# A decoder layer on one core: ordered first statistics in twelve 92-token tiles, three buffers moved, a 256-token last block

## The chip, the cores and the metric

The kernel runs on one core of a Trainium2 chip. A core has TensorE (PE in the profile, with its weight loads as PEld), VectorE (DVE), ScalarE (ACT), GpSimd (POOL) and SyncE (SP), which issues the DMAs here; 16 DMA engines move the data. The metric is device microseconds for one launch: lower is better. Clock means the clock that was granted to TensorE, 1.00 for 2.4 GHz and 0.50 for 1.2 GHz.

## The reference

One decoder layer over 1104 tokens: 16 learned meta tokens and a prompt of 1024 tokens (one sequence of 1040), and 8 sampled sequences of 8 tokens. The model is 1024 wide.

```python
def decoder_layer(x, st, p):
    x = x + 0.5 * swiglu(rmsnorm(x, p['ffn1_norm']), p['ffn1_w_gu'], p['ffn1_w_down'])   # 1024 -> 2 x 2816 -> 1024
    u = rmsnorm(x, p['mix_norm'])
    z = u @ p['w_in']
    # A gated DeltaNet, B S5 (complex diagonal state), C RG-LRU, D GLU + causal depthwise conv31 + LayerNorm; each 256 wide
    ...
    gates = jax.nn.sigmoid(zg.reshape(*zg.shape[:-1], N_BRANCH, D_MODEL))
    x = x + jnp.sum(gates * proj, axis=-2) @ p['w_out']
    x = x + 0.5 * swiglu(rmsnorm(x, p['ffn2_norm']), p['ffn2_w_gu'], p['ffn2_w_down'])
```

y_prompt (without the meta tokens) and y_sample are the RMSNorm of x with final_norm. The new states of the four branches are outputs too.

## The kernel before

Activations lie with the 1024 (or 2816) channels on the partitions and tokens along the free dimension. Every float32 product is made of three passes of a narrower type (hi times hi, hi times lo, lo times hi), so a weight tile `raw` is split by a cast on ACT into `whi` and a subtraction on DVE into `wlo`, and so are the activations. The framework's scheduler sets the order on each engine by its own simulation of the times; `high_priority` and `issue_after` steer it. On each engine, and on SP's queue, instructions then run in that order, and one that waits holds back all that stand behind it. A pool tile has a tag and a number of buffers; a new tile of a tag waits until an old one is no longer read.

The stages are FFN 1, the norm of the mixers (`norms`), the input projection with the four branches woven into it, the merge, FFN 2 and the final norm.

- **Start of FFN 1.** The input arrives with tokens on partitions, in ten tiles: 16 meta tokens, eight of 128 tokens and one of 64. PE turns each in eight transposes (`turn_x`, into `xs`), and ACT or DVE sum the squares of each row (`stats_x`, with an rsqrt and three Newton steps on DVE: `rsqrt_rows`). PE spreads the row factors `y` over all partitions into `rs`. `scale` multiplies by `rs` and the norm weight, and a split into hi and lo gives the factor `b` that the matmuls read. FFN 1 works in token blocks of 276; the first one needs tokens from four tiles, the first four loaded. The gate and up products of the first four units (of 128 of the 2816 channels) are made plainly, for the token blocks 0 and 1: units 0 and 1, then 2 and 3, each pair 96 matmuls for a block. All later work uses seven products of sums for every eight (`a_prep` adds the weights, `b_first` and `b_rest` the activations). `a_prep` takes three raw tiles, `r1`, `r2` and `s23`, of which the last two come from the pool `gw` with two buffers.
- **norms** keeps two accumulators per token block of 368, one of them a `raw` tile of the weight pool. The first tile of w_in is loaded into the next free `raw`.
- **Delta rule (branch A).** `scale_q` is called for three token blocks and multiplies the queries `a_qe` by decays that a DMA spreads over the partitions into `a_bc`: two rows of 368 numbers, each to 64 partitions, 184 KB. It does so twice for a block, six times in all, on POOL. `a_bc` shares its one buffer (tag `n_acc0`) with other work, `b_sg` of S5 among it. A chunk of the rule takes `a_mt`, `a_tk` from DRAM, `a_wT` from ACT and `a_kd` from POOL.
- **Conv (branch D)** multiplies by a tap on ACT into `d_tmp` (one buffer) and adds on POOL into `d_acc`.
- **S5 (branch B)** has four steps q; each does input matmuls (`b_mi`), a scan on DVE, and output matmuls (`b_H` with `b_mo`). A `yield` lets a piece of the input projection (24 matmuls of 368 columns) go between.
- **down** adds the last group of units' outputs in three token blocks of 368; after each, `final` transposes the tokens of that block back, three outputs of up to 128 tokens, and normalises and stores them. The third output of each block uses the tile `fy`, with one buffer.

Of the kernel before, what the change touches and what calls it, by code (L numbers as in the profile page):

```python
# [13 lines left out]
D = 1024  # L14
# [12 lines left out]
NS = 276  # L27
NF = DFF // 128
# [14 lines left out]
class Kernel:  # L43
# [52 lines left out]

    def split(self, hi, lo, x, eng=None):
        self.nc.scalar.copy(out=hi, in_=x)  # L98
        (eng or self.nc.vector).tensor_tensor(out=lo, in0=x, in1=hi.bitcast(F32), op=SUB)  # L99

    def rsqrt_rows(self, ps, out, tmp):

        nc = self.nc
        nc.scalar.activation(out=out, in_=ps, func=AF.Abs_reciprocal_sqrt, bias=self.eps[:ps.shape[0]])
        nc.vector.scalar_tensor_tensor(out=tmp, in0=ps, scalar=EPS, in1=out, op0=ADD, op1=MULT)
        nc.vector.scalar_tensor_tensor(out=tmp, in0=tmp, scalar=-0.5, in1=out, op0=MULT, op1=MULT)
        nc.vector.scalar_tensor_tensor(out=out, in0=tmp, scalar=1.5, in1=out, op0=ADD, op1=MULT)

    def norms(self, key, after=None, tbs=range(3)):
# [166 lines left out]
    def tokens(self):  # L276

        I = self.I
        blocks = [(I["meta_tokens"], NMETA, 0)]
        for i in range(8):  # L280
            blocks.append((I["x_prompt"][0, 128 * i:128 * i + 128], 128, NMETA + 128 * i))
        return blocks + [(I["x_sample"].rearrange("b t d -> (b t) d"), TS, TP)]

    def load_x(self, tiles, pools):

        ts = []
        for i, n in enumerate(tiles):
            src, r, c0 = self.tokens()[n]
# [3 lines left out]
            ts.append((xin[:, i % 2], r, c0))  # L292
        return ts

    def turn_x(self, ts, xs, pools, tags, eng):

        nc = self.nc
        for t, r, c0 in ts:
            for h in range(2):
# [4 lines left out]
                for b in range(c0 // NS, (c0 + r - 1) // NS + 1):  # L304
                    if b not in xs:
                        xs[b] = self.slot(pools[b], "xs", F32, (8, NS))
                    lo, hi = max(c0, NS * b), min(c0 + r, NS * (b + 1))
                    dst, src = xs[b][:, 4 * h:4 * h + 4, lo - NS * b:hi - NS * b], ps[:, :, lo - c0:hi - c0]
                    if h and eng:
                        nc.vector.tensor_copy(out=dst, in_=src)  # L310
                    else:
                        nc.scalar.copy(out=dst, in_=src)

    def stats_x(self, ts, pool, tag):
# [5 lines left out]
        for i, (t, r, c0) in enumerate(ts):  # L320
            if pool and i % 2 == 0:
                junk = self.slot(pool, "junk", F32, (2, D))
            sq = junk[:r, i % 2] if pool else t[:r]
            if i == 1 and c0 < NS:
# [13 lines left out]
        nc.scalar.activation(out=self.rs[:, ts[0][2]:ts[0][2] + n], in_=ps[:, :n], func=AF.Copy, scale=float(D))  # L338
# [18 lines left out]
    def scale(self, dst, src, b, ks=range(8)):  # L357

        for k in ks:
            self.nc.vector.scalar_tensor_tensor(out=dst(k), in0=src(k), in1=self.rs[:, NS * b:NS * (b + 1)], op0=MULT,  # L360
                                                scalar=self.prm[:, self.po[self.gkey] + k:self.po[self.gkey] + k + 1], op1=MULT)
# [41 lines left out]
    def a_parts(self, f, rs):  # L403

        pool, out = (self.wp, self.gw)[f % 2], []
        for r in rs:
            h, l = (pool.tile([128, 8, 128], F32R, tag=x, name=x, bufs=3 if pool is self.wp else None) for x in ("whi", "wlo"))
            self.split(h, l, r)
# [28 lines left out]
    def gate_up(self, w_in, parts):  # L437
# [60 lines left out]
        def plain(f, A, t, ea):  # L498
# [9 lines left out]
            for i in range(2):  # L508
                product(ps[i], A[i][1], B[6 if t else 1], False)
                with self.tc.high_priority():  # L510
                    if t:
                        nc.vector.tensor_tensor(out=g[:, i], in0=ps[i], in1=ea[i], op=ADD)
                    if i == 0:
                        nc.scalar.activation(out=g[:, 0], in_=g[:, 0] if t else ps[0], func=AF.Silu)
# [10 lines left out]
        with self.tc.high_priority():  # L525
# [1618 lines left out]
```

## Time and profile before

| | us |
|---|---|
| Median of 3 runs | 2610.69 (2607.91 to 2612.38) |
| Profiled execution, its own time | 2605.56 |
| Its span in the profile | 2603.9 |
| PE busy | 2531.2 (97%), mean clock 0.981 |
| DVE, ACT, POOL busy | 1458.5, 912.7, 534.7 |

The profiled execution took 1.66 us more than its span, and lies 5.13 us under the median. Times in the trace are counted from the start of the span.

### The profile page before, as it was taken

The numbers are of one execution on the slowest core, as the hardware profiler recorded it, in microseconds if no ns is written. First come the engines' busy times: TensorE is split into PE (matmuls) and PEld (weight loads), VectorE is DVE, ScalarE is ACT, GpSimd is POOL, SyncE is SP. The second block draws the span as 40 slices with busy tenths as digits, with TensorE's granted clock in tenths as the row PEclk, the third lists the DMA queues.
The fourth block names the chain that finished last, engine by engine and source line by source line (L and its number), as shares of the span: only waits on it lengthen the run. The fifth ranks groups of instructions, "written<-read, shape, count | busy, mean of one in ns | idle before, by whom it ended". The sixth has DMA issues, their size and how long they took to land.

```text
span 2603.9 us, 43522 instructions
## 1 busy us (share of the span) xinstructions
PE 2531.2 (97%) x17474; PEld 2459.5 (94%) x17474; DVE 1458.5 (56%) x2729; ACT 912.7 (35%) x1665; POOL 534.7 (21%) x578
## 2 busy tenths in 40 slices
PE   7999999999999999989999999999999999999997
PEld 7999999999998898888989999999999999999997
DVE  6645444656787459687744335343855444464545
ACT  7433333421224355334523213132533333341203
POOL 1222222200002021144443222221232222210000
PEclk8999999999999999989989999999999999999999
DMA  7222222542413243633433536242222222362211
GB/s 230 77 76 92 76 76 76 199 145 82 127 68 108 78 79 121 135 97 109 128 111 97 189 101 216 87 136 93 72 87 92 76 79 79 101 216 83 103 48 69
DMA packets 317224, 280.68 MB, mean 108 GB/s; under 512 B 62708, under 2 KB 276078, under 8 KB 316886
## 3 DMA queue, kind: packets, MB, share of 16 engines
q1 hardware_dynamic: 317021, 277.90, 34.8%
q8 instruction: 137, 2.24, 0.4%
q14 instruction: 66, 0.53, 0.1%
HBM read 196.31 MB, written 81.72 MB: 107 GB/s over the span
## 4 chain that ended last, share of the span: by engine, by line
PE 83%; DVE 7%; DMA 4%; ACT 3%; issue 2%; POOL 1%; SPq 1%; POOLq 0%; DVEq 0%; ACTq 0%
PE ps_mm L59 63%; PE ps_pre L59 7%; PE ps_vn L59 6%; PE ps_o L59 6%; DVE wlo L99 1%; PE ps_P L59 1%; PE ps_pre L67 1%; DMA a_bc<-qsP 0%; DVE d_acc L783 0%; DVE b L99 0%; DVE b_t L1650 0%; ACT whi L98 0%; DVE x L578 0%; DMA tokS<-a_tok 0%; DMA raw<-in_ffn_w_gu 0%
## 5 line engine op out<-in xcount | busy, mean ns | idle before, releaser
L59 PE MATMUL ps_mm<-u,whi 128*128 128x368 f32 (+1 forms) x2816 | 719.1, 336 | 8.5 <-ACT whi L98 4.3
L59 PE MATMUL ps_mm<-h,whi 128*128 128x368 f32 x2112 | 529.2, 332 | 3.7 <-DVE x L578 3.5
L59 PEld LDWEIGHTS ps_mm<-u,whi 128*128 128x128 f32 x2816 | 504.2, 191 | 23.4 <-issue 5.7
L98 ACT CAST whi<-raw 128x1024 fp32r<-128x1024 f32 (+2 forms) x305 | 299.5, 986 | 607.6 <-PE ps_mm L59 414.8
L59 PE MATMUL ps_mm<-u,wlo 128*128 128x368 f32 (+1 forms) x1408 | 469.4, 334 | 0.0
L59 PE MATMUL ps_mm<-b,whi 128*128 128x276 f32 x2816 | 447.9, 291 | 6.3 <-ACT b L98 3.2
L99 DVE TENSOR_TENSOR wlo<-raw,whi 128x1024 fp32r<-128x1024 f32 (+2 forms) x305 | 387.0, 1273 | 102.9 <-ACT whi L98 102.1
L59 PEld LDWEIGHTS ps_mm<-b,whi 128*128 128x128 f32 x2816 | 393.3, 189 | 7.8 <-ACT b L98 3.8
L59 PEld LDWEIGHTS ps_mm<-h,whi 128*128 128x128 f32 x2112 | 374.0, 188 | 7.4 <-DVE x L578 6.2
L59 PE MATMUL ps_mm<-h,wlo 128*128 128x368 f32 x1056 | 349.4, 332 | 0.0
L59 PEld LDWEIGHTS ps_mm<-u,wlo 128*128 128x128 f32 x1408 | 268.0, 190 | 3.4 <-issue 2.0
L578 DVE SCALAR_TENSOR_TENSOR x<-ps_mm,x 128x368 f32<-128x368 f32 x288 | 154.4, 538 | 173.3 <-PE ps_mm L59 172.0
L59 PE MATMUL ps_mm<-b,wlo 128*128 128x276 f32 x1408 | 237.6, 290 | 0.0
L59 PEld LDWEIGHTS ps_mm<-b,wlo 128*128 128x128 f32 x1408 | 201.4, 189 | 0.1
L59 PEld LDWEIGHTS ps_mm<-h,wlo 128*128 128x128 f32 x1056 | 198.3, 188 | 0.3
L144 DVE TENSOR_TENSOR g_sg<-ps_mm,rs 128x368 f32<-128x368 f32 x96 | 51.8, 539 | 202.0 <-PE ps_mm L59 201.8
L427 POOL TENSOR_TENSOR raw<-raw 128x512 f32<-128x512 f32 x44 | 57.2, 1301 | 519.0 <-DVE wlo L99 499.7
L59 PE MATMUL ps_pre<-b,whi 128*128 128x276 f32 x896 | 145.5, 291 | 0.0
L59 PEld LDWEIGHTS ps_pre<-b,whi 128*128 128x128 f32 x896 | 127.1, 190 | 0.0
L1821 ACT ACTIVATE g_sg<-g_sg 128x368 f32<-128x368 f32 x96 | 48.9, 509 | 211.3 <-DVE g_sg L144 211.3
L466 DVE TENSOR_TENSOR e_g<-ps_pre,e_a 128x276 f32<-128x276 f32 x80 | 35.4, 443 | 154.6 <-DMA hS<-e_g 133.7
L489 POOL TENSOR_TENSOR e_g<-e_g,e_u 128x276 f32<-128x276 f32 x80 | 99.2, 1240 | 77.2 <-issue 35.3
(488 smaller groups left out, 3385.1 us busy)
## 6 DMA issues: line engine op xcount, KB each, us to landing
raw<-in_ffn_w_gu SPq DMA_DIRECT2D x104, 512.0 KB
raw<-in_w_in SPq DMA_DIRECT2D x50, 512.0 KB
h<-hS SPq DMA_DIRECT2D x44, 552.0 KB
hS<-e_g SPq DMA_DIRECT2D x80, 276.0 KB
raw<-in_ffn_w_down SPq DMA_DIRECT2D x38, 512.0 KB
x<-xS SPq DMA_DIRECT2D x24, 552.0 KB
mgS<-g_mg SPq DMA_DIRECT2D x24, 552.0 KB
g_b<-brS SPq DMA_DIRECT2D x16, 552.0 KB
```

The lines of the kernel that those rows point to most:

```text
L59: self.last_mm = self.nc.tensor.matmul(out=out, lhsT=lhsT, rhs=rhs, start=start, stop=stop, **kw).ins
L67: self.last_mm = self.nc.tensor.transpose(out=out, in_=in_, identity=self.ident[:n, :n]).ins
L98: self.nc.scalar.copy(out=hi, in_=x)
L99: (eng or self.nc.vector).tensor_tensor(out=lo, in0=x, in1=hi.bitcast(F32), op=SUB)
L144: self.last_dve = self.nc.vector.tensor_tensor(out=out, in0=ps, in1=r, op=MULT).ins
L427: nc.gpsimd.tensor_tensor(out=s23[:, k2], in0=r1[:, k1], in1=r2[:, k1], op=SUB)
L466: add(out=g[:, 0], in0=gam, in1=e["a"], op=ADD)
L489: nc.gpsimd.tensor_tensor(out=g[:, 1], in0=g[:, 1], in1=e["u"], op=MULT)
L578: nc.vector.scalar_tensor_tensor(out=x[:, m, sl], in0=ps, scalar=0.5, in1=x[:, m, sl], op0=MULT, op1=ADD)
L1821: self.last_act = nc.scalar.activation(out=sg, in_=sg, func=AF.Tanh, scale=0.5).ins
```

## The change

Seven edits, in the order of the program.

1. The input's 1104 tokens come in twelve tiles of 92, three to a block of 276 (`tokens`, `load_x`). The first of them is a load of 16 and one of 76 tokens, the last one of 28 and one of 64. The first block's three tiles are loaded first, then the first unit's weights, three tiles, the second unit's weights, and the last six tiles.
2. The statistics are ordered: `issue_after` keeps the splits of the first two units' weights, the second block's transposes and the first silu behind steps of the statistics. `y` itself, spread over 128 columns, is the stationary operand of the matmul that gives `rs`; the diagonal matrices go away, and so does the factor 1024. The first factor is made in two halves. The second block's rows are turned and its statistics made while the first block is at work (`next_rows`). Half of the last six tiles' copies go to DVE, and their statistics come in two groups of three.
3. `s23` of the first seven-product unit comes from the pool `wp` with the other raw tiles.
4. `norms` takes both accumulators from the pool `tp`, and no `raw`.
5. `a_bc` has a tag, and so a buffer, of its own.
6. S5: the two scan tiles become one that shares its buffer with `b_y`; one of the yields moves from ahead of the input matmuls to ahead of the output matmuls (1 and 4 in place of 2 and 3).
7. The last group of FFN 2's down product ends its blocks at tokens 400, 848 and 1104; `final` has 3, 4 and 2 outputs for them, two buffers of `fy`, and cycles through five PSUM places.

```diff
+NT = NS // 3
...
-                acc = [self.raw([128, NB]),
-                       pool.tile([128, NB], F32, tag="f_s", name="n_acc")]
+                acc = [pool.tile([128, NB], F32, tag="f_s", name="n_acc") for _ in range(2)]
...
+        xp, xs = I["x_prompt"][0], I["x_sample"].rearrange("b t d -> (b t) d")
+        c = NT * n - NMETA
+        out = []
+        if c < 0:
+            out.append((I["meta_tokens"], 0))
+        a, b = max(c, 0), min(c + NT, TP - NMETA)
+        out.append((xp[a:b], a - c))
+        if b < c + NT:
+            out.append((xs, b - c))
+        return out
...
-            self.nc.sync.dma_start(out=xin[:r, i % 2], in_=src)
+            for src, o in self.tokens(n):
+                self.nc.sync.dma_start(out=xin[o:o + src.shape[0], i % 2], in_=src)
...
-            dg = self.tp.tile([128, 128], F32, tag="f_h", name="xdg")
-            nc.scalar.activation(out=dg[:r, :r], in_=self.ident[:r, :r], func=AF.Copy, scale=y[:r, i:i + 1])
-            self.mm(ps[:, n:n + r], self.onesD[:r], dg[:r, :r])
+            self.mm(ps[:, n:n + r], y[:r, i:i + 1].to_broadcast([r, 128]), self.ident[:r, :r])
...
-            self.split(h, l, r)
+            with self.after(*b):
+                self.split(h, l, r)
...
-            r1, r2, s23 = (self.raw([128, 8, 128], pool) for pool in (None, self.gw, self.gw))
+            r1, r2, s23 = (self.raw([128, 8, 128], pool) for pool in (None, self.gw, None if f == self.NP else self.gw))
...
-        blocks = [[(16, 128), (144, 128), (272, 96)], [(368, 128), (496, 128), (624, 112)],
-                  [(736, 128), (864, 128), (992, 112)]][tb]
+        blocks = [[(16, 128), (144, 128), (272, 128)], [(400, 128), (528, 128), (656, 128), (784, 64)],
+                  [(848, 128), (976, 128)]][tb]
...
-            yt = self.raw([128, 2, 512]) if i < 2 else fp.tile([128, 2, 512], F32, tag="fy", name="fy")
+            yt = self.raw([128, 2, 512]) if i < 2 else fp.tile([128, 2, 512], F32, tag="fy", name="fy", bufs=2)
...
-                bc = self.np.tile([128, NB], F32, tag="n_acc0", name="a_bc")
+                bc = self.np.tile([128, NB], F32, tag="a_bc", name="a_bc")
...
-            yield
-            Sr, Si = (pool.tile([128, 2, NBLK], F32, tag=f"b_S{m}", name="b_S") for m in range(2))
+            S = pool.tile([128, 2, 2, NBLK], F32, tag="b_S", name="b_S")
+            Sr, Si = S[:, 0], S[:, 1]
...
-            ys = pool.tile([128, 4, NBLK], F32, tag="b_y", name="b_y")
+            ys = pool.tile([128, 4, NBLK], F32, tag="b_S", name="b_y")
             early = inputs(q + 1) if q < 3 else None
-            yield
-            yield
-            yield
+            for _ in range(4):
+                yield
...
+                    us["rs"], us["mm"], us["st"] = self.last_rs, self.last_mm, (self.last_rt, self.last_nr)
+                    self.hold = [(us["st"], (self.last_rs, self.last_nr))]
...
+                def next_rows():
+                    ts = us["ts"]
+                    with self.after(us["scaled"], us["rs"], us["mm"]):
+                        self.turn_x(ts, xs, [v] * 4, ("P", "o"), True)
+                    with self.after(*us["st"]):
+                        self.stats_x(ts, up, "vn")
...
-                    self.down(I["ffn2_w_down"], start, None, self.final)
+                    self.down(I["ffn2_w_down"], start, None, self.final, (400, 848, T))
```

The scheduler sets the order anew. On PE, this is the end of the first statistics and the first FFN matmuls in the kernel before (`ps_vn` is the spreading of the row factors; a `DMAHW` in the brackets is the load that the row waits for).

```order
L59 MATMUL ps_vn<-xdg,onesD 128x16 [waits Activation_49]
L59 MATMUL ps_vn<-xdg,onesD 128x128 [waits Activation_49] x3
L67 MATMUL ps_P<-ident,xin 128x128 [waits DMAHW5_49,PE_49,Activation_49]
L67 MATMUL ps_P<-ident,xin 128x128 x3
L67 MATMUL ps_o<-ident,xin 128x128 [waits DVE_49]
L67 MATMUL ps_o<-ident,xin 128x128 x3
L67 MATMUL ps_P<-ident,xin 128x128 [waits DMAHW6_49,Activation_49]
L67 MATMUL ps_P<-ident,xin 128x128 x3
L59 MATMUL ps_mm<-b_244,whi 128x276 [waits Activation_49]
```

And in the changed kernel:

```order
L60 MATMUL ps_vn<-ident,x_s 128x92 [waits DVE_49]
L60 MATMUL ps_vn<-ident,x_s 128x92 x2
L68 MATMUL ps_P<-ident,xin 128x92 [waits DMAHW1_49,PE_49]
L68 MATMUL ps_P<-ident,xin 128x92 x3
L68 MATMUL ps_o<-ident,xin 128x92 x4
L68 MATMUL ps_P<-ident,xin 128x92 [waits DMAHW2_49,Activation_49]
L68 MATMUL ps_P<-ident,xin 128x92 x3
L60 MATMUL ps_mm<-b_216,whi 128x276 [waits Activation_49]
```

In both, transposes of later tiles stand ahead of the first FFN matmul: in the changed kernel those of the fourth tile and half of the fifth.

On POOL, the first two multiplications by `a_bc` of the kernel before stand together ahead of the conv's additions, and the other four far behind:

```order
L1238 TENSOR_TENSOR a_qe<-a_qe,a_bc 128x368 [waits DMAHW3_49,DMAHW2_49,DMAHW4_49,DMAHW1_49,DMAHW6_49,DVE_49,Activation_49]
L1238 TENSOR_TENSOR a_qe<-a_qe,a_bc 128x368 [waits DMAHW3_49]
L797 TENSOR_TENSOR d_acc<-d_acc,d_tmp 128x368 [waits Activation_49] x2
L797 TENSOR_TENSOR d_acc<-d_acc,d_tmp 128x304 [waits Activation_49]
```

In the changed kernel the last four are these, and two more stand shortly ahead of them:

```order
L1260 TENSOR_TENSOR a_qe<-a_qe,a_bc 128x368 [waits DMAHW7_49]
L1291 TENSOR_TENSOR a_kd<-a_tk,a_kdT 40x256 [waits DMAHW6_49,PE_49]
L1260 TENSOR_TENSOR a_qe<-a_qe,a_bc 128x368 [waits DMAHW0_49]
L1260 TENSOR_TENSOR a_qe<-a_qe,a_bc 128x368 [waits DMAHW4_49,DMAHW3_49]
L1260 TENSOR_TENSOR a_qe<-a_qe,a_bc 128x368 [waits DMAHW6_49,DMAHW5_49]
L819 TENSOR_TENSOR d_acc<-d_acc,d_tmp 128x368 [waits DVE_49,Activation_49]
L819 TENSOR_TENSOR d_acc<-d_acc,d_tmp 128x368 [waits Activation_49]
```

All six stand within a stretch of 17 of POOL's rows now, among additions of the conv. On ACT of the changed kernel, the taps that these additions take stand as follows (the second row here waits for the first addition that stands behind the four multiplications):

```order
L818 ACTIVATE d_tmp<-d_buf,prm_5929 128x368 [waits Pool_49]
L1302 COPY a_vn<-ps_vn 40x256 [waits PE_49]
L818 ACTIVATE d_tmp<-d_buf,prm_5929 128x368 [waits Pool_49]
L818 ACTIVATE d_tmp<-d_buf,prm_5929 128x304 [waits Pool_49]
L818 ACTIVATE d_tmp<-d_buf,prm_5929 128x64
L1842 ACTIVATE g_sg<-g_sg 128x368 [waits DVE_49]
L1324 COPY a_qe<-ps_o 128x2x40 [waits PE_49]
L1332 COPY a_wT<-ps_pre 128x80 [waits PE_49]
```

Behind them stand a gate (`g_sg`), and `a_wT`, which PE's next chunk of the delta rule reads.

## Rows read from the trace of the kernel before

**Rows 1.** Page, busy time of an engine, share of the span and instructions.

```profile
PE 2531.2 (97%) x17474; PEld 2459.5 (94%) x17474; DVE 1458.5 (56%) x2729; ACT 912.7 (35%) x1665; POOL 534.7 (21%) x578
```

**Rows 2.** Stretches: length; PE, PEld, DVE, ACT, POOL busy; clock, DMA share, GB/s.

```profile
60.00:80.00 20.00, 20.00 (x156) 19.71 (x155) 18.91 (x30) 9.03 (x16) 1.69 (x1) 1.00 0.27 79
80.00:100.00 20.00, 16.09 (x110) 15.87 (x110) 15.20 (x16) 9.70 (x13) 8.46 (x5) 0.86 0.11 36
800.00:820.00 20.00, 15.70 (x76) 15.15 (x76) 11.89 (x19) 6.95 (x13) 7.15 (x24) 0.83 0.45 117
1220.00:1240.00 20.00, 15.79 (x106) 15.20 (x104) 11.18 (x18) 7.85 (x15) 8.59 (x10) 0.95 0.41 119
1240.00:1260.00 20.00, 19.28 (x109) 18.77 (x110) 12.20 (x18) 9.89 (x20) 9.17 (x11) 0.88 0.38 116
```

**Rows 3.** Timeline of PE, 24 to 100: start, length; in brackets idle before.

```profile
25.32 1.16 PE L59 MATMUL ps_mm<-b,whi 128*128 128x276 f32 x4
...
44.30 1.29 PE L59 MATMUL ps_mm<-b,whi 128*128 128x276 f32 x4 [3.16 <-ACT b L98]
...
59.58 0.76 PE L59 MATMUL ps_mm<-b,whi 128*128 128x276 f32 x4
...
95.19 1.28 PE L59 MATMUL ps_vn<-b,whi 128*128 128x276 f32 x4 [3.91 <-ACT whi L98]
```

**Rows 4.** Timeline of SP's queue, the first loads of the input.

```profile
2.31 1.36 SPq L291 DMA_DIRECT2D xin<-in_x_prompt  x3
```

**Rows 5.** Three short stretches, columns as in rows 2.

```profile
4.50:6.00 1.50, 0.59 (x6) 0.49 (x6) 0.23 (x1) 0.21 (x1) 0.00 (x0) 1.00 1.00 382
...
1235.00:1239.00 4.00, 0.79 (x5) 0.49 (x3) 1.98 (x3) 0.56 (x2) 1.10 (x2) 0.87 0.12 44
1339.00:1339.60 0.60, 0.60 (x6) 0.60 (x5) 0.10 (x1) 0.00 (x0) 0.00 (x0) 1.00 0.52 153
```

**Rows 6.** Timeline of SP's queue, loads of a_tk and a_bc.

```profile
1139.00 0.32 SPq L1255 DMA_DIRECT2D a_tk<-tokS  x1
...
1225.03 8.89 SPq L1235 DMA_DIRECT2D a_bc<-qsP  x2
```

**Rows 7.** Timeline of POOL, the two multiplications that take them.

```profile
1231.40 1.98 POOL L1238 TENSOR_TENSOR a_qe<-a_qe,a_bc 128x368 f32<-128x368 f32 x1 [2.64 <-DMA a_bc<-qsP]
...
1239.11 0.96 POOL L1238 TENSOR_TENSOR a_qe<-a_qe,a_bc 128x368 f32<-128x368 f32 x1 [3.01 <-DMA a_bc<-qsP]
```

**Rows 8.** Timeline of ACT, a copy that waited for POOL.

```profile
1127.51 0.23 ACT L1302 COPY a_qe<-ps_o 128x80 f32<-128x80 f32 x1 [7.67 <-POOL a_qe L1238]
```

**Rows 9.** Timeline of PE, four places in the mixers' stages.

```profile
805.47 2.21 PE L59 MATMUL ps_mm<-u,whi 128*128 128x368 f32 x6 [4.30 <-ACT whi L98]
...
1082.80 0.50 PE L59 MATMUL ps_mm<-u,whi 128*128 128x368 f32 x2
1083.13 0.33 PE L59 MATMUL ps_mm<-u,wlo 128*128 128x368 f32 x1
...
1089.50 0.80 PE L59 MATMUL ps_pre<-b_H,b_mo 128*128 128x138 f32 x2 [5.07 <-issue]
...
1159.94 0.64 PE L59 MATMUL ps_vn<-a_tk,a_mt 40*40 40x64 f32 x8
...
1240.72 0.68 PE L59 MATMUL ps_pre<-b_yh,whi 128*128 128x368 f32 x1 [4.93 <-ACT b_sg L1777]
```

**Rows 10.** Timelines of SP and ACT, the first tile of w_in.

```profile
799.84 0.38 SPq L82 DMA_DIRECT2D raw<-in_w_in  x1
...
804.37 1.04 ACT L98 CAST whi<-raw 128x1024 fp32r<-128x1024 f32 x1 [1.23 <-DMA raw<-in_w_in]
```

**Rows 11.** Timeline of all engines at the end.

```profile
2586.63 0.54 DVE L578 SCALAR_TENSOR_TENSOR x<-ps_mm,x 128x368 f32<-128x368 f32 x1
...
2595.58 0.69 DVE L619 TENSOR_TENSOR fy<-ps_mm,fg 112x512 f32<-112x512 f32 x1 [1.67 <-DMA out_y_prompt<-fy]
...
2599.91 0.57 SPq L630 DMA_DIRECT2D out_y_sample<-fy  x1
```

More of the change, by code (lines that the diff above doesn't have):

```diff
@@ L273, in col, with tokens @@
         return prm[:, o:o + 1]
-    def tokens(self):
+    def tokens(self, n):
         I = self.I
[L279 to L282, printed above, removed]
+        xp, xs = I["x_prompt"][0], I["x_sample"].rearrange("b t d -> (b t) d")
[8 more added lines that the diff above has]
+        return out
     def load_x(self, tiles, pools):
@@ L303, in turn_x, with stats_x @@
                     self.transpose(ps[:, j, :r], t[:r, k * 128:k * 128 + 128], r)
[L304 to L314, printed above, removed]
+                b, o = divmod(c0, NS)
+                if b not in xs:
+                    xs[b] = self.slot(pools[b], "xs", F32, (8, NS))
+                dst, src = xs[b][:, 4 * h:4 * h + 4, o:o + r], ps[:, :, :r]
+                if h and eng:
+                    nc.vector.tensor_copy(out=dst, in_=src)
+                else:
+                    nc.scalar.copy(out=dst, in_=src)
+    def stats_x(self, ts, pool, tag, dve=True):
         nc = self.nc
@@ L401, in a_load, with a_parts @@
         return rs
-    def a_parts(self, f, rs):
+    def a_parts(self, f, rs, behind=((), ())):
         pool, out = (self.wp, self.gw)[f % 2], []
-        for r in rs:
+        for r, b in zip(rs, behind):
             h, l = (pool.tile([128, 8, 128], F32R, tag=x, name=x, bufs=3 if pool is self.wp else None) for x in ("whi", "wlo"))
-            self.split(h, l, r)
+            with self.after(*b):
+                self.split(h, l, r)
             out.append([(h[:, k], l[:, k]) for k in (slice(0, 4), slice(4, 8))])
@@ L513, in plain @@
                     if i == 0:
-                        nc.scalar.activation(out=g[:, 0], in_=g[:, 0] if t else ps[0], func=AF.Silu)
+                        with self.after(*(self.silu or ())):
+                            nc.scalar.activation(out=g[:, 0], in_=g[:, 0] if t else ps[0], func=AF.Silu)
             if t:
@@ L525, in gate_up @@
         with self.tc.high_priority():
+            self.hold, self.silu = [], None
             raws = todo[0]()
-            A = [self.a_parts(f, raws[f]) for f in range(2)]
+            A = [self.a_parts(0, raws[0], *self.hold[:1])]
+            todo[1]()
+            A.append(self.a_parts(1, raws[1], *self.hold[1:]))
+        todo = todo[1:]
         for f0 in range(0, self.NP, 2):
@@ L564, in load_h, with down @@
         return hs
-    def down(self, wd_in, start, hook=None, after=None):
+    def down(self, wd_in, start, hook=None, after=None, ends=(NB, 2 * NB, T)):
         nc = self.nc
@@ L571, in down, with out @@
         x = self.x = Rows([self.slot(self.v, "x", F32) for _ in range(4)])
-        def out(hs, w, m, tb):
-            sl = slice(tb * NB, (tb + 1) * NB)
-            ps = self.psum([128, NB])
+        def out(hs, w, m, sl):
+            ps = self.psum([128, sl.stop - sl.start])
             for i, (hh, hl) in enumerate(hs):
@@ L590, in down @@
                     for tb in range(3):
-                        out(hs, [[t[:, i, 128 * (m % 2):][:, :128] for t in w] for i in range(len(fs))], m, tb)
+                        out(hs, [[t[:, i, 128 * (m % 2):][:, :128] for t in w] for i in range(len(fs))], m,
+                            slice(tb * NB, (tb + 1) * NB))
                 if hook:
@@ L594, in down @@
         ws = [self.weights(wd[:, f:f + 1], 1, 1024) for f in groups[-1]]
-        for tb in range(3):
+        for b, end in enumerate(ends):
             for m in range(8):
-                out(nxt, [[t[:, 0, 128 * m:128 * m + 128] for t in w] for w in ws], m, tb)
+                out(nxt, [[t[:, 0, 128 * m:128 * m + 128] for t in w] for w in ws], m, slice((0, *ends)[b], end))
             if after:
-                after(tb)
+                after(b)
     def final(self, tb):
@@ L1978, in fourth @@
                     ts = us["ts2"]
[L1979 to L1980 removed]
+                    self.turn_x(ts, xs, [v] * 4, ("P", "o"), True)
+                    for i in (0, 3):
+                        self.stats_x(ts[i:i + 3], None, "vn", False)
                     keep(2)
@@ L1993, in fifth @@
                     self.b_rest(1, xs[2], xs[3], u22, tmp, homes[1])
-                return first, second, fourth, third, fifth
+                return first, next_rows, second, fourth, third, fifth
             es_cm = ExitStack()
@@ L2104, in fourth @@
                     self.b_rest(1, u2, u3, u22, tmp, homes[1])
-                return first, second, third, fourth
+                return first, (lambda: None), second, third, fourth
             with ffn(I["ffn2_w_gu"], I["ffn2_w_down"], parts) as start:
```

60 lines of the change are left out of this document (37 added, 23 removed).

## The prediction

> **What bounds the kernel now.** I read the page first: PE is busy for 97% of the span [rows 1], so time can only be won where PE waits or runs at the lower clock. Then I went through the span in stretches of 20 us and took length minus busy time times clock as the loss of a stretch. Some 109 us are lost in all, most of them in few places, and the change touches five of these: 80 to 100 loses 20 - 16.09 x 0.86 = 6.2, 800 to 820 loses 7.0, 1220 to 1260 loses 5.0 + 3.0 [rows 2], and the start, S5's first output and the end I read from the timeline, as the wait in brackets before a matmul. PE's first FFN matmul starts at 25.32; the second token block starts at 44.30 after a wait of 3.16, the third unit at 59.58; the first seven-product unit waits 3.91 at 95.19 [rows 3]. The waits of 4.30, 5.07 and 4.93 in the mixers' stages stand in [rows 9].
>
> **Start (edits 1 to 3).** The order of the statistics saves work on ACT and DVE ahead of the first matmul. But the loads change their shape, and this I price first. Tiles of 128 rows kept all 16 DMA engines busy (share 1.00) at 382 GB/s, which is 23.9 GB/s for an engine, 0.171 us for a row of 4 KB. Loads of 40 rows (a_mt and a_tk) ran at a share of 0.52, eight engines, 18.4 GB/s each; a_bc with its two source rows at 0.12, two engines [rows 5]. The two 40-row loads were under way together at that 0.52, so they shared the same eight. Equal parts give just that: 40 rows in fives over 8, 2 over 2, 128 over 16. 92 rows in equal parts fit on at most 4 engines. If engines were filled row by row instead, 92 would use at least 12. I take 4, since the 40 rows did not use 10 or more.
>
> The Trainium skill, "DMA: Bandwidth & Descriptors", section "Why a DMA increments its semaphore by 16 and not by 1", states that such a load runs on the largest number of engines up to 16 that divides the slowest dimension of both sides, and on the lowest-numbered ones. By it 92 and 76 rows get 4 engines, the same 4 for every tile, and the sum is the one worked out here; with all 16 it would be 13 us lower. [...]
>
> So the first four engines carry for the first three tiles 1 + 19 + 23 + 23 = 66 rows, 11.3 us. From about 3.0 (the middle of the issue at 2.31 [rows 4]) that is 14.3. Two weight tiles of 512 KB at 382 GB/s: 17.0. Tiles 4 and 5: 24.9; tile 6: 28.8; the second unit's weights: 31.5; tile 7: 35.4; tiles 8 to 12: 52.2; then a store of 1104 KB and the third unit's weights, 5.7, and a cast of 1.04: about 59. PE runs in order. Its first FFN matmul stands behind half of the fifth tile: about 26, so nothing is won against 25.32. It then stops for tile 6 at 28.8, for the second unit's weights at 33 and for tile 7 at 35.4. At that point 64 of the first block's 96 matmuls are left, 0.128 each (20 us over 156 [rows 2]), 8.2, with 3 for the low clock and 2 for transposes: 49, and the second block's 96 take 12.3. With a dozen more transposes the third unit starts near 63, 3 later than 59.58; the 28 transposes still to come cost 3, and the wait at 95.19 with its clock is won, 6.2, since the first seven-product unit takes its third raw tile elsewhere. Sum 0. The lower end is -5 (if ACT and DVE have the second block's factor early and the low clock is short). For the upper end I take the 18.4 GB/s of the 40-row loads: 0.223 a row, 256 rows, the weights at 76: +13. I stay with 0.171, measured on rows of the same 4 KB.
>
> **norms (edit 4).** The first w_in tile was issued at 799.84, when a `raw` came free, and its cast began at 804.37 [rows 10]; PE waited 4.30. Now nothing holds a `raw` there, so it is loaded earlier, and the cast waits only for the last `whi` to be free, about 800. 7.0 are lost in that stretch; I take 5, between 0 (another wait steps in) and 7.
>
> **a_bc (edit 5).** The wait of 4.93 at 1240.72 goes with its clock, 8.0: S5's `b_sg` no longer waits for the buffer. But all six multiplications now stand close together on POOL, the last three with nothing between. The new buffer is still one, so each load waits for the multiplication before. One turn took 1239.11 - 1231.40 = 7.7 [rows 7], of which 1.0 was a longer multiplication; I take 7.3 with the next issue (two issues lie 8.89 apart and end [rows 6]). The third load stands behind one of a_tk that PE releases, at 1139.00 [rows 6], 4 earlier with what S5 wins: 1135. Four turns end at 1135 + 29.2 = 1164. Behind them on POOL are the conv's additions, and ACT, with its one `d_tmp`, waits at the tap for them; behind the tap stand the gate and `a_wT`, another 4 us: 1168. PE wants that `a_wT` where chunk 4's matmuls began, 1159.94 [rows 9], less 4: 1156. PE waits 12, and 3 more go in low clock; some 4 come back from waits on DVE that the pause absorbs. +11 against -8: +3. That POOL holds ACT in this way shows in [rows 8], 7.67 us for one such load. Lower end -8: no wait, if the first four multiplications come early. If the third load goes right after the second multiplication, near 1127, the wait is 12 - 8 = 4.
>
> **S5 (edit 6).** PE waited 5.07 for the first `b_H` with 72 matmuls of the projection for cover. Now 24 more stand there, at (1083.13 - 1082.80) / 2 = 0.167 us [rows 9]: 4.0. The input matmuls of the next step lose 16 of cover for a load; I take -4, between -6 (with the clock) and -1.
>
> **End (edit 7).** The last main matmul's sum is taken at 2586.63 [rows 11]; 17.3 follow. A wait of 1.67 for the store of `fy` goes, and so does one output of three. But the block before now gives four outputs, in a last block of 256 columns that lasts only 8 x 6 x 0.119 = 5.7 (0.167 x 256/368 = 0.116 a matmul), and its DVE work of some 2.6 an output lies partly behind the end. -4, between -6.5 and +1.
>
> Edits with no term: order, half of the copies on DVE (18.91 of 20 busy at 60 to 80 [rows 2], so no room there, but the tiles also come later).
>
> **Sum.** 0 - 5 + 3 - 4 - 4 = -10. Of the profiled execution's 2605.56 (span 2603.9 and 1.66) that leaves 2595.6; the median of the runs is 5.13 higher, 2610.69, and I give the time on its scale: 2600.7. About 0.2%, 5.2 us, is what a measurement of this kernel can tell from no change.
>
> **The rivals.**
> - *The tiles of 92 take all 16 engines.* Then the first three land by 8, and the chain of the first statistics (15 us from load to first matmul before) is shortened: start -13. Total -23, 2587.7. For it: DMA share 0.52 is an average. Against it: two shapes fit equal parts.
> - *The a_bc chain stays hidden*: ACT reaches the tap later than I think. Total -21, 2589.7. Both together: -34, 2576.7.
> - *Slower: the a_bc chain holds PE throughout.* If ACT is stopped already at the second load, as in [rows 8], PE gets no work into the five turns of 36.5 beyond some 10, and with the clock it loses 29 in place of 11: total +8, 2618.7. The point from which it decides: a pause of PE over 26 us between 1120 and 1190.
> - *The waits reappear*: norms, S5 and the end give half: -3.5, 2607.2, no change that can be told.
>
> **How the numbers follow.** Forecast 0.42 (own range 2589 to 2613: 0.30 of it faster, 0.09 the same, 0.03 slower), all engines 0.15, hidden chain 0.15, both 0.04, slower 0.10, reappearing 0.14 (0.11 the same, 0.03 slower). Faster 0.30 + 0.15 + 0.15 + 0.04 = 0.64; same 0.20; slower 0.16. The range from 2585 to 2617 leaves out the case of both, most of the slower one and the tails of the others, about 0.2.
>
> **What would show it.** Right: a DMA share near 0.25 while the 92-row tiles load; the first FFN matmul near 26 and the third unit near 63; no wait at the first seven-product unit; w_in's cast close to 800; a wait of ACT at a tap of the conv with four `a_qe` multiplications some 7 us apart, and a pause of PE of about 12 behind it; none at `b_sg`; a last stretch of 13 in place of 17.3. Wrong: a first FFN matmul near 15, or multiplications 3 us apart, would make it faster than I say; a third unit past 70 or a pause past 25 slower.

## The result, and the profile after

The changed kernel takes 2634.27 us (median of 4 runs, 2633.46 to 2638.88), the kernel before beside it 2609.30 (2607.08 to 2612.38): ratio 1.0098, 95% interval 1.0081 to 1.0116. It is slower by 25 us, where I forecast 2600.7 and gave 2617 as the upper end. The profiled execution of after is the longest of its four (2638.88, span 2637.1), that of before is 3.7 us below its median; so the 33 us between the two traces stand for 25 between the medians.

The page of after has, answering to [rows 1], nearly the same busy times over a longer span, and one group of matmuls whose idle time (last column, with its main releaser) stands out:

```profile
PE 2531.0 (96%) x17494; PEld 2457.2 (93%) x17494; DVE 1464.5 (56%) x2740; ACT 910.2 (35%) x1656; POOL 539.7 (20%) x579
...
L60 PE MATMUL ps_mm<-b,whi 128*128 128x276 f32 x2816 | 453.1, 293 | 25.5 <-ACT e_a L521 16.1
```

PE is busy for 2531 us in both, so the loss is time in which PE is idle. To find where, I took the first start of matmuls that mark stages and compared them:

| PE's first ... | before | after | later by |
|---|---|---|---|
| FFN matmul (b, whi) | 25.3 | 28.4 | 3.1 |
| matmul of FFN1's second half (h, whi) | 507.0 | 532.3 | 25.3 |
| product with w_in (u, whi) | 805.5 | 830.2 | 24.7 |
| matmul of c_xf | 950.0 | 972.9 | 22.9 |
| b_H of S5 | 1089.5 | 1108.4 | 18.9 |
| a_mt, a_vn of the chunks | 1112.8 | 1139.0 | 26.2 |
| b_yh of S5's gate | 1224.5 | 1257.0 | 32.5 |
| a_wq | 1531.3 | 1560.2 | 28.9 |
| statistics of FFN2 (rs, onesD) | 1817.8 | 1846.6 | 28.8 |
| last matmul of FFN2's first half (b) | 2326.7 | 2363.6 | 36.9 |
| last matmul with h | 2586.1 | 2625.7 | 39.6 |
| end of the span | 2603.9 | 2637.1 | 33.2 |

So the start costs 25.3, all of it before 140 us (in windows of 10 us no loss of more than 1 us follows up to 507). PE's timeline of after there, answering to [rows 3], with the tiles' landings ahead:

```profile
8.93 0.84 PE L68 MATMUL ps_mm<-ident,xin 92*128 92x92 f32 x4 [5.54 <-DMA xin<-in_x_prompt]
12.41 0.87 PE L68 MATMUL ps_mm<-ident,xin 92*128 92x92 f32 x4 [2.02 <-DMA xin<-in_x_prompt]
16.80 0.57 PE L68 MATMUL ps_mm<-ident,xin 92*128 92x92 f32 x2 [3.51 <-DMA xin<-in_x_prompt]
...
28.39 0.81 PE L60 MATMUL ps_mm<-b,whi 128*128 128x276 f32 x2
...
62.63 1.29 PE L60 MATMUL ps_mm<-b,whi 128*128 128x276 f32 x4 [16.14 <-ACT e_a L521]
...
69.51 0.78 PE L60 MATMUL ps_mm<-b,whi 128*128 128x276 f32 x4 [0.16 <-ACT b L107]
...
82.39 0.76 PE L60 MATMUL ps_mm<-b,whi 128*128 128x276 f32 x4
...
125.17 0.78 PE L60 MATMUL ps_mm<-b,whi 128*128 128x276 f32 x4 [2.60 <-DVE b L108]
127.32 0.88 PE L60 MATMUL ps_mm<-b,whi 128*128 128x276 f32 x4 [1.36 <-ACT whi L107]
```

Tiles follow each other by 3.5 and 4.4 us, as four engines give (3.9 worked out). But there is a wait of 16.14 in the middle; the second block starts at 69.51 in place of 44.30, and the third unit at 82.39 in place of 59.58, 22.8 late. PE waits for the copy e_a; ACT's timeline says why it is late:

```profile
61.24 1.04 ACT L107 CAST whi<-raw 128x1024 fp32r<-128x1024 f32 x1 [18.89 <-DMA raw<-in_ffn_w_gu]
62.20 0.38 ACT L521 COPY e_a<-ps_mm 128x276 f32<-128x276 f32 x1
62.48 0.39 ACT L350 COPY rs<-ps_vn 128x276 f32<-128x276 f32 x1
...
68.34 1.12 ACT L107 CAST b<-bt 128x1104 fp32r<-128x1104 f32 x1
69.36 1.11 ACT L107 CAST b<-ub 128x1104 fp32r<-128x1104 f32 x1
```

The cast at 61.24 is that of the third unit's first weight tile. It waits 18.89 us for its load, which lands at 61 (58 worked out, 59 with the cast). ACT runs in order: behind it stand e_a and rs of the first two blocks and the second block's factors (the last two rows), and PE wants all of these long before the third unit.

The windows bear out the engines (columns as in [rows 2]; share and GB/s last). The stretch 8 to 13 of before, then of after:

```profile
8.00:13.00 5.00, 2.62 (x16) 1.81 (x14) 3.97 (x8) 5.00 (x11) 0.00 (x0) 0.95 1.12 341
```

```profile
8.00:13.00 5.00, 2.05 (x12) 1.80 (x12) 0.54 (x1) 0.47 (x1) 0.00 (x0) 1.00 0.28 104
50.00:60.00 10.00, 0.00 (x0) 0.00 (x0) 0.00 (x0) 0.00 (x0) 0.00 (x0) 0.50 0.56 170
```

A share of 0.28 is 4.5 engines of 16, with some weights in it; from 10 to 12, with the tiles alone, it is 0.25, four engines, at 102 GB/s. The Trainium skill, "DMA: Bandwidth & Descriptors", section "Why a DMA increments its semaphore by 16 and not by 1", has it that a load runs on the largest number up to 16 that divides the slowest dimension of both its sides, here the rows; for 92 the trace now agrees. The second row shows the price: nothing is busy for 10 us, and PE's clock has gone to the lower level.

For 40 rows the same rule gives ten engines.

The prediction read eight for them from a share of 0.52, but the trace of before has ten. Beside the packets that carry rows it counts small ones of under 512 B: 16 where tiles of 128 rows load at a share of 1.00 (4.5 to 6), 2 for a load of a_bc at 0.12 (1235 to 1239), and in after 4 where tiles of 92 rows load at 0.25 (22 to 26). That is one for each engine. The two loads of 40 rows have 20 together (1338.9 to 1340.3), so ten each. The 4 engines for 92 rows were right, but the reason given for taking 4, "since the 40 rows did not use 10 or more", was a misreading, and so there was luck in it.

In the mixers' stages the chain of a_bc went as worked out. POOL's multiplications, then ACT at the conv's tap, then PE (answering to [rows 7, 8, 9]):

```profile
1168.82 1.02 POOL L1260 TENSOR_TENSOR a_qe<-a_qe,a_bc 128x368 f32<-128x368 f32 x1 [3.48 <-DMA a_bc<-qsP]
...
1176.09 1.33 POOL L1260 TENSOR_TENSOR a_qe<-a_qe,a_bc 128x368 f32<-128x368 f32 x1 [5.48 <-DMA a_bc<-qsP]
1183.88 0.96 POOL L1260 TENSOR_TENSOR a_qe<-a_qe,a_bc 128x368 f32<-128x368 f32 x1 [6.46 <-DMA a_bc<-qsQ]
1192.62 0.96 POOL L1260 TENSOR_TENSOR a_qe<-a_qe,a_bc 128x368 f32<-128x368 f32 x1 [7.77 <-DMA a_bc<-qsQ]
1193.54 0.96 POOL L819 TENSOR_TENSOR d_acc<-d_acc,d_tmp 128x368 f32<-128x368 f32 x1
```

```profile
1194.53 0.60 ACT L818 ACTIVATE d_tmp<-d_buf,prm 128x368 f32<-128x368 f32 x1 [19.34 <-POOL d_acc L819]
```

```profile
1197.68 1.07 PE L60 MATMUL ps_vn<-a_S,a_wT 128*40 128x128 f32 x4 [12.88 <-ACT a_wT L1332]
```

The turns are 7.3 to 8.7 us (7.3 forecast), the pause 12.88 (12 forecast), and at b_sg 1.2 us are waited in place of 4.93 [rows 9].

S5 was not as forecast. The first b_H comes without a wait, 4.0 relative to before earlier (22.9 to 18.9 in the table). But a new wait stands right behind it. PE, then SP's queue of after:

```profile
1108.44 0.40 PE L60 MATMUL ps_pre<-b_H,b_mo 128*128 128x138 f32 x2
...
1124.21 2.18 PE L60 MATMUL ps_pre<-b_ur,b_mi 128*128 128x138 f32 x8 [8.61 <-issue]
```

```profile
1110.54 1.31 SPq L1267 DMA_DIRECT2D a_el<-elP  x2
1115.87 0.31 SPq L1185 DMA_DIRECT2D qsQ<-sp  x1
...
1117.60 0.35 SPq L1685 DMA_DIRECT2D b_ur<-uS  x1
```

and SP's queue of before at the same place in the program:

```profile
1092.17 0.35 SPq L1663 DMA_DIRECT2D b_ur<-uS  x1
...
1095.61 0.37 SPq L1163 DMA_DIRECT2D qsQ<-sp  x1
```

Before, the next step's b_ur was loaded ahead of the store of qsQ. Now it stands behind it, and qsQ waits in the queue for DVE (SP issues nothing from 1111.85 to 1115.87). The input matmuls that use b_ur have been moved forward, so nothing is left to cover it.

### The profile page after: what moved, and what is told of

Its sections match the earlier page's. It is cut to its first block, busy times and chain, and to the rows that moved or that the text cites. A ratio compares the mean times of both kernels' runs of the same rounds, so it can differ in the third digit from the quotient of the medians.

```text
span 2637.1 us, 43568 instructions
## 1 busy us (share of the span) xinstructions
PE 2531.0 (96%) x17494; PEld 2457.2 (93%) x17494; DVE 1464.5 (56%) x2740; ACT 910.2 (35%) x1656; POOL 539.7 (20%) x579
## 5 line engine op out<-in xcount | busy, mean ns | idle before, releaser
L60 PE MATMUL ps_mm<-h,whi 128*128 128x368 f32 (+3 forms) x2112 | 531.0, 333 | 3.9 <-DVE x L597 3.9
L60 PEld LDWEIGHTS ps_mm<-u,whi 128*128 128x128 f32 x2816 | 502.3, 190 | 18.6 <-issue 5.8
L60 PE MATMUL ps_mm<-h,wlo 128*128 128x368 f32 (+3 forms) x1056 | 350.6, 333 | 0.0
L597 DVE SCALAR_TENSOR_TENSOR x<-ps_mm,x 128x368 f32<-128x368 f32 (+3 forms) x288 | 154.3, 538 | 177.0 <-PE ps_mm L60 175.4
```

The lines of the kernel that those rows point to most:

```text
L60: self.last_mm = self.nc.tensor.matmul(out=out, lhsT=lhsT, rhs=rhs, start=start, stop=stop, **kw).ins
L597: nc.vector.scalar_tensor_tensor(out=x[:, m, sl], in0=ps, scalar=0.5, in1=x[:, m, sl], op0=MULT, op1=ADD)
```

## The experiments

**The start.** Theory 1: the start's loss comes from loads on four engines, by way of the cast on which ACT stands. First, the loads alone were cut so that 16 divides their greater part:

```diff
-                self.nc.sync.dma_start(out=xin[o:o + src.shape[0], i % 2], in_=src)
+                m = src.shape[0] // 16 * 16
+                for a, b in ((0, m), (m, src.shape[0])):
+                    if b > a:
+                        self.nc.sync.dma_start(out=xin[o + a:o + b, i % 2], in_=src[a:b])
```

> The changed kernel, with each load of input tokens cut in two at the largest multiple of 16 rows (92 as 80 and 12, 76 as 64 and 12, 28 as 16 and 12); tiles and order stay. Theory 1: the start loses some 21 us because a load of 92 or 76 rows runs on 4 DMA engines only, so that the third unit's weights land at 61 us and their cast holds ACT, with everything PE wants behind it. Then the wait of 16.1 us at 62.6 us goes, the x tiles land in some 15 us instead of 45, and the time falls by 20 to 30 us: 2604 to 2614. Rival: the order of the statistics and the waits set for it hold PE, whatever the loads do. Then the time stays within 5 us of 2634, and the wait before unit 1 remains over 10 us.

Measured: 2617.61 us, ratio 1.0034 (1.0021 to 1.0047), 17 less than after: three or four us above the expectation, and still slower than before. The stretch from 26 to 30, with cut tiles alone under way, shows all engines at work (FFN1's second half starts at 518.6 in place of 532.3):

```profile
26.00:30.00 4.00, 2.25 (x18) 2.03 (x19) 1.59 (x3) 3.02 (x6) 0.00 (x0) 1.00 1.03 248
```

What is left is again the third unit's cast, on ACT's and PE's timelines:

```profile
38.32 1.04 ACT L107 CAST whi<-raw 128x1024 fp32r<-128x1024 f32 x1 [8.88 <-DMA raw<-in_ffn_w_gu]
39.27 0.29 ACT L113 ACTIVATE x_s<-x_s,eps 128x4 f32<-128x4 f32 x1
```

```profile
41.14 1.59 PE L60 MATMUL ps_vn<-ident,x_s 92*128 92x92 f32 x6 [7.28 <-DVE x_s L117]
```

Then the start was taken alone, with the norms' accumulators, a_bc's buffer, S5's order and the last blocks of before:

```diff
-                acc = [pool.tile([128, NB], F32, tag="f_s", name="n_acc") for _ in range(2)]
+                acc = [self.raw([128, NB]),
+                       pool.tile([128, NB], F32, tag="f_s", name="n_acc")]
...
-                bc = self.np.tile([128, NB], F32, tag="a_bc", name="a_bc")
+                bc = self.np.tile([128, NB], F32, tag="n_acc0", name="a_bc")
...
-                    self.down(I["ffn2_w_down"], start, None, self.final, (400, 848, T))
+                    self.down(I["ffn2_w_down"], start, None, self.final)
```

> The kernel before with the edits of the start alone (tiles of 92, the order of the statistics, the first unit's tile from the other pool); the accumulators of the norms, a_bc's buffer, S5's order and the last blocks are as before. If the start is worth +21 and the rest of the change about 0 to +4 (a_bc +5, norms and end -4 each, second FFN +10 by the profile), then 2609 + 21 = 2630, and 2640 if the 10 us that the second FFN's start lost in the profile come from the first unit's tile. Rival: the loss is spread over the later edits, and the start alone is under +12: below 2621.

Measured: 2639.86, ratio 1.0115 (1.0099 to 1.0131). The start alone costs 30 us, and the rest of the change wins 4 to 6 of these back. In its trace PE is 25.8 late at FFN1's second half.

Next, with the slow loads left as they are, the cast was held on ACT behind the second block's rs:

```diff
-            self.hold, self.silu = [], None
+            self.hold, self.silu, self.rs1 = [], None, ()
...
-                    A = [self.a_parts(f, self.a_load(w, f)) for f in fs]
+                    A = [self.a_parts(f, self.a_load(w, f), (self.rs1 if f == 2 else (), ())) for f in fs]
...
-                    self.silu = [self.last_rt]
+                    self.silu, self.rs1 = [self.last_rt], (self.last_rs,)
```

> The changed kernel with its slow loads as they are; only the cast of the third unit's first weight tile is held on ACT until the second block's rs copy is issued, so that ACT does the first block's e_a and the second block's rs copies before it waits for these weights. Theory 1 with its way: the tiles of 92 rows are late, but PE loses its 16.1 us because ACT stands at that cast. Then e_a and rs come at about 45 us, block 1 starts near 48 to 52 instead of 69.5, the third unit near 63 to 66 as the prediction had it, and the time falls by 8 to 15 us: 2619 to 2626. Rival: PE's own order is what holds it (three transposed tiles of the third block stand ahead of block 1, and they land late); then the wait only changes its name and the time stays within 4 us of 2634.

Measured: 2637.5, ratio 1.0100 (1.0085 to 1.0116): nothing won. ACT's and PE's timelines show that the hold was too weak to test the theory: rs moved ahead of the cast, but an e_a copy still stood behind it.

```profile
44.65 0.39 ACT L350 COPY rs<-ps_vn 128x276 f32<-128x276 f32 x1 [0.36 <-PE ps_vn L60]
60.85 1.04 ACT L107 CAST whi<-raw 128x1024 fp32r<-128x1024 f32 x1 [15.82 <-DMA raw<-in_ffn_w_gu]
...
62.85 0.37 ACT L521 COPY e_a<-ps_pre 128x276 f32<-128x276 f32 x1
```

```profile
63.28 1.29 PE L60 MATMUL ps_pre<-b,whi 128*128 128x276 f32 x4 [15.83 <-ACT e_a L521]
```

So it was held behind the second block's factor casts instead:

```diff
                     self.b_first(0, us[0], us[1], us[1][:, 4:8], tmps[0], homes[0], (0, 1))
+                    self.rs1 = (self.last_hi,)
...
-                    self.silu, self.rs1 = [self.last_rt], (self.last_rs,)
+                    self.silu = [self.last_rt]
```

> The changed kernel, token loads as they are, with the third unit's first weight cast held on ACT until the second block's factor casts are issued (the weaker hold left one e_a copy, three xs copies and the factor casts behind it, and won nothing). Theory 1 with its way (PE loses 16 us because ACT stands at a cast whose weights land at 61, with work for block 1 behind it): block 1 starts near 50 instead of 69.5, the wait of 16 us goes or falls under 4, the third unit starts at 63 to 67, and the time falls by 9 to 16 us: 2618 to 2625. Rival: late tokens, not the place of the cast, set the start: PE waits for tiles of the third block or for the weights themselves as long, and the time stays within 4 us of 2634.

Measured: 2626.63, ratio 1.0064 (1.0052 to 1.0076), 8 to 9 less than after, just short of the 9 to 16 that were expected. PE's timeline shows the wait of 16 gone and the second block at 52.77 in place of 69.51; but part of that is given back at 72.72:

```profile
52.77 0.77 PE L60 MATMUL ps_mm<-b,whi 128*128 128x276 f32 x4 [0.16 <-ACT b L107]
...
65.64 0.76 PE L60 MATMUL ps_mm<-b,whi 128*128 128x276 f32 x4
...
72.72 1.26 PE L60 MATMUL ps_pre<-b,whi 128*128 128x276 f32 x4 [5.31 <-DVE e_g L526]
```

```profile
70.64 0.45 DVE L526 TENSOR_TENSOR e_g<-ps_mm,e_a 128x276 f32<-128x276 f32 x1 [3.15 <-DMA hS<-e_g]
```

PE waits there for DVE (second fence, DVE's timeline), and DVE for the store of an earlier e_g, which is issued on SP behind the late loads. On ACT the next unit's first cast waits at the same time for its weights:

```profile
72.56 1.04 ACT L107 CAST whi<-raw 128x1024 fp32r<-128x1024 f32 x1 [5.66 <-DMA raw<-in_ffn_w_gu]
```

Then both remedies together, once with the weak hold and once with the strong one (a_bc's loads are in both as two of 64 rows, whose edit stands below; they come long after the start):

> The changed kernel with the token loads cut at multiples of 16 rows, a_bc's loads as two of 64 partitions, and the third unit's cast held behind the second block's rs copy. If the three are separate losses, 2617.6 - 9 - 7 (PE's wait of 7.3 us for the second block's statistics at 41 us, behind that cast) = 2602, faster than before. Rival: with all 16 engines the hold wins nothing, since PE then waits for the weights itself: 2608.

> The kernel with the cut token loads and a_bc as two loads, with the stronger hold of the third unit's cast (behind the second block's factor casts) in place of the weaker. With all 16 engines these weights land near 38 us; the weaker hold still had PE wait 2.3 us for an e_a copy behind that cast. If that is all that is left there, 2598; if the later cast now makes the third unit wait, 2602.

Measured: 2600.3, ratio 0.9967 (0.9953 to 0.9980), and 2602.32, 0.9973 (0.9961 to 0.9985). The two can't be told apart, and both are faster than before, by 0.3%. FFN1's second half starts at 508.2 with the strong hold (510.1 with the weak), so that the four cases of loads and strong hold are 25.3, 19.4, 11.6 and 1.2 us later than before:

| | cast as in the change | cast held |
|---|---|---|
| loads on 4 engines | 25.3 | 19.4 |
| loads on 16 engines | 11.6 | 1.2 |

So the hold is worth 6 with the slow loads and 10 with the cut ones, and the cut loads are worth 14 without the hold and 18 with it. Of these 18, 10 stand already at the first FFN matmul (28.05 against 18.08), and the other 8 are those of the wait at 72.72.

One loss is in all four. PE's timeline of the kernel with both remedies has, shortly behind the start of the first seven-product unit, the same two waits that after has at 125.17 and 127.32:

```profile
99.76 0.78 PE L60 MATMUL ps_mm<-b,whi 128*128 128x276 f32 x4 [2.58 <-DVE b L108]
101.90 1.29 PE L60 MATMUL ps_mm<-b,whi 128*128 128x276 f32 x4 [1.37 <-ACT whi L107]
```

The start is not late there, so they do not come from slow loads. DVE, for whose factor PE waits, is busy for 9.70 of the 10 us from 90 to 100, and for 10.00 from 110 to 120 in after.

**The first seven-product unit's tile** (edit 3), in the pool of before, in the changed kernel and in the one with loads, a_bc and weak hold:

```diff
-            r1, r2, s23 = (self.raw([128, 8, 128], pool) for pool in (None, self.gw, None if f == self.NP else self.gw))
+            r1, r2, s23 = (self.raw([128, 8, 128], pool) for pool in (None, self.gw, self.gw))
```

> The changed kernel with the first seven-product unit's third weight tile in the pool of before. Both FFNs use that code. If the second FFN's new waits (e_b 1.9 us, e_u 1.6 us) come from that tile, its part falls from +8 to about +4 or less against before, and the first FFN gets a wait of some 4 us back or not: 2628 to 2636. Rival: the second FFN's waits stay (+4 to +8) whatever the pool: 2634 to 2640.

> As the kernel with the cut token loads, a_bc as two loads and the held cast, and the first seven-product unit's third weight tile in the pool of before too. If that tile costs the second FFN 4 us and wins nothing in the first: 2598; if it wins in the first FFN what it costs in the second: 2602; if only the first FFN feels it: 2606.

Measured: 2642.16, ratio 1.0126 (1.0112 to 1.0140), and 2608.17, 0.9998 (0.9989 to 1.0007). The tile of the other pool wins 7 to 8 us both times, in the first FFN; the later start of the second FFN's first half is not its doing.

**a_bc** (edit 5). Its old buffer first, then its own buffer with loads of 64 rows:

```diff
-                bc = self.np.tile([128, NB], F32, tag="a_bc", name="a_bc")
+                bc = self.np.tile([128, NB], F32, tag="n_acc0", name="a_bc")
```

> The changed kernel with a_bc in the buffer it had before, shared with b_sg. Theory 2: the six loads of a_bc in a row through a buffer of their own hold POOL, and with it ACT and PE, for 12.9 us and the low clock behind it, some 15; with the old buffer that goes, and the wait of 8 us with its clock at b_sg comes back: 2634 - 15 + 8 = 2627, 3 to 10 us below the changed kernel. Rival: the pause has another cause (the order of the gates), then nothing is won and b_sg's wait comes on top: 2634 to 2642.

Measured: 2629.46, ratio 1.0076 (1.0063 to 1.0089), 5 to 6 less than after, within the 3 to 10 of theory 2 (the two intervals just overlap). PE's wait at the delta rule falls from 12.88 to 1.0, and b_sg's is back (two of PE's waits between 1112 and 1320: us in total, times, longest):

```profile
PE ps_pre L60 <- ACT b_sg L1798: 5.3, 1, 5.3
PE ps_vn L60 <- ACT d_tmp L818: 1.0, 1, 1.0
```

```diff
-                        self.dq.dma_start(out=dst, in_=bass.AP(tensor=s.tensor, offset=s.offset + 2 * pr * n + o,
-                                                               ap=[[n, 2], [0, 64], [1, dst.shape[1]]]))
+                        for h in range(2):
+                            self.dq.dma_start(out=dst[64 * h:64 * h + 64],
+                                              in_=bass.AP(tensor=s.tensor, offset=s.offset + (2 * pr + h) * n + o,
+                                                          ap=[[0, 64], [1, dst.shape[1]]]))
```

> The changed kernel with each load of a_bc issued as two loads of 64 partitions, one source row each, so that the slowest dimension of each is 64 and not 2. Theory 2 with its reason (two DMA engines carry a load of 184 KB, some 4 us of each turn of 7.3): a turn falls to 3 to 5 us, ACT's wait of 19.3 us at the conv's tap falls under 8, PE's pause of 12.9 goes, and the time falls by 10 to 16 us: 2618 to 2624. Rival: a turn is made of the issue, the multiplication and the queue in front of SP, not of the load's engines; then turns stay above 6 us and the time within 3 us of 2634.

Measured: 2625.85, ratio 1.0057 (1.0044 to 1.0070), 8 to 11 less than after. PE's pause is gone, but not for the reason given. POOL's timeline has turns of 6.5 and 6.4 us, where 3 to 5 were expected, and the conv's additions now go behind the fifth multiplication, 12 us earlier than behind the sixth:

```profile
1167.40 1.81 POOL L1262 TENSOR_TENSOR a_qe<-a_qe,a_bc 128x368 f32<-128x368 f32 x1 [1.85 <-DMA a_bc<-qsP]
...
1173.95 1.17 POOL L1262 TENSOR_TENSOR a_qe<-a_qe,a_bc 128x368 f32<-128x368 f32 x1 [4.16 <-DMA a_bc<-qsP]
1180.36 0.96 POOL L1262 TENSOR_TENSOR a_qe<-a_qe,a_bc 128x368 f32<-128x368 f32 x1 [5.23 <-DMA a_bc<-qsQ]
1181.28 0.96 POOL L819 TENSOR_TENSOR d_acc<-d_acc,d_tmp 128x368 f32<-128x368 f32 x1
...
1188.19 0.96 POOL L1262 TENSOR_TENSOR a_qe<-a_qe,a_bc 128x368 f32<-128x368 f32 x1 [1.41 <-DMA a_bc<-qsQ]
```

So of theory 2 it is shown that the chain of six multiplications on a_bc's buffer, with the conv's additions behind it, holds PE; that two engines' speed makes the turns is not. The rival was right on the turns and wrong on the time.

**S5's order** (edit 6; SP's and PE's timelines below), put back in the kernel with loads, a_bc and weak hold:

```diff
+            yield
             S = pool.tile([128, 2, 2, NBLK], F32, tag="b_S", name="b_S")
...
-            for _ in range(4):
+            for _ in range(3):
                 yield
```

> The kernel with the cut token loads, a_bc as two loads and the held cast (2600.3 us), with S5's steps at the places of before; the shared buffer of b_S and b_y stays. Theory 3: S5's new order puts the load of b_ur on SP behind the store of qsQ, which waits 4.1 us for DVE, so that it is issued 25 us later in the stretch than before and PE waits 9.6 us for it; the old order has b_H's wait of 5.1 us instead. Then the wait of 9.6 goes, one near 5 comes, and the time falls by 3 to 6 us: 2594 to 2597. Rival: the wait has to do with the shared buffer of b_S and b_y, not with the order: it stays above 8 us and the time within 2 us of 2600.

Measured: 2604.07, ratio 0.9981 (0.9971 to 0.9992): 3 to 6 us were to be won, and it is 4 slower, though the intervals overlap; against the kernel with the strong hold, which ran on the same chip, it is 2 slower. So nothing was won, and a loss is not shown. The wait did move as expected: b_ur is loaded ahead of qsQ again (SP), and b_H waits instead (PE):

```profile
1096.58 0.34 SPq L1690 DMA_DIRECT2D b_ur<-uS  x1
1099.54 0.37 SPq L1188 DMA_DIRECT2D qsQ<-sp  x1
```

```profile
1093.91 0.80 PE L60 MATMUL ps_pre<-b_H,b_mo 128*128 128x138 f32 x2 [6.44 <-issue]
```

Between the matmul of c_xf and that of a_mt and a_vn the old order falls behind the kernel before by 1.4 us and the new one by 3.6, so 2 are won there. From a_mt to the last gate of S5 the new order then gains 9.5 us on the kernel before and the old one 1.7. Which wait makes that difference is not settled: there are several of 1 to 3 us in the old order, none of them large.

## Why the prediction was wrong, by its own steps

**Start, 0 forecast, +25.3 in the trace.** The landings were nearly right (tiles 3.9 us apart, third unit's weights at 61 for 58), and the first FFN matmul came at 28.4 for 26. The step that failed is the one behind "At that point 64 of the first block's 96 matmuls are left": from there I let PE wait for its own operands alone, put the second block's 96 matmuls at 49 and the third unit at 63, 3 late. They start at 69.51 and 82.39, 22.8 late. I priced the late weights only where PE uses them, and never looked at what stands behind their cast on ACT. Held behind the second block's factors, with the same loads, the wait of 16.14 goes and the third unit does start at 65.6. But the late loads have more ways to PE than this one: with the cast held the start is still 19.4 late, 8 of it by the wait at 72.72, where a store and weights stand behind the late tiles, and that was not in the sum either.

A second piece of the sum failed too, the 6.2 that were to be won at the first seven-product unit. They are won and lost again. Counting matmuls with b, the one after 400 others starts 25.0 later than in before, after 460 others 18.7, after 520 others 24.8: the wait of 3.91 is gone, and 2.60 and 1.36 with their clock have come shortly behind it. They stand in the kernel with both remedies too, so they are no part of the late start. PE waits there mostly for DVE; the half of the copies that edit 2 gave to DVE had no term in the sum, but whether they are the cause no run shows. Edit 3 in itself was priced well: -6.2 forecast, 7 to 8 measured against the same start without it.

**norms, -5 forecast, -2.4 in the table** (25.3 to 22.9; the kernel with the start alone goes from 25.8 to 26.5 there, so 3 against it). The load of w_in did move forward, but PE now waits 2.15 for DVE's sum at 817, which was in the bounds (0 to 7).

**a_bc, +3 forecast, +5 to 6 measured**, by the mechanism and with the pause (12.88 for 12) that the text gave. The term was a little small.

**S5, -4 forecast with -1 as the worst.** The 4.0 are there at the first b_H; what the text called "16 of cover for a load" cost 8.6 us of wait and not 3, because the load's place in SP's queue was not looked up. At a_mt PE is 26.2 late in place of 22.9: +3.3. The experiment on the order did not give these back, so on the whole of the mixers' stages the sign of this edit stays open.

**End, -4 forecast, -3.7 in the table**: +2.7 up to the last matmul with h, then -6.4; the last stretch from DVE's last sum, at 2626.22 in after, is 10.9 us in place of 17.3 [rows 11].

**Not in the sum:** FFN2's first half, +8.1 in the profile of after. In the profiles of the experiments it is 2.4 to 8.5, in the kernel with the start alone 3.6, so some 3 us of it come with the start's edits, though not with edit 3, as its experiments show; what else moves them there is not settled. The rest may be a matter of this one execution: the two traces differ by 8 us more than the medians.

Of the rivals, the one with 16 engines and the hidden a_bc chain are refuted, as is a pause over 26 us; none of them had the wait that decided. With 16 engines by cut loads, the first matmul comes at 18.6, but even with the cast held the kernel's start is not faster than before, where that rival had 13 us. The rival of the waits that reappear had part of it: norms, S5 and the end bring -2.4, +3.3 and -3.7 in the table, -2.8 for a forecast of -13.

## What to carry to other kernels

When a load gets later, look up what stands behind its first consumer on that in-order engine, not only who uses the data: here a weight cast that waited for its load stood ahead of copies for which PE waited 16 us. Loads of 92 rows, which 16 does not divide, ran on four DMA engines: cutting 92 into 80 and 12 won 17 us. And whoever moves a step forward must follow its loads through the queue; a store that waits for another engine holds every load behind it.

## What the runs showed that was not expected

The cut loads fill all engines, but move less than tiles of 128 rows: 248 GB/s at a share of 1.03 from 26 to 30, where before moves 382 at 1.00 from 4.5 to 6 [rows 5]; why is open. The last twelve are issued in 12.38 us; whether issuing or moving them takes that time is not shown:

```profile
17.72 12.38 SPq L309 DMA_DIRECT2D xin<-in_x_prompt  x12
```

And a load of a_bc on more engines wins little: from the end of one multiplication to the start of the next 6.25 us (1169.84 to 1176.09) became 4.74 (1169.21 to 1173.95), issue included.
